# Late-search counts and the attention's squares: from VectorE to ScalarE

## The chip, the cores and the metric

The kernel runs as one program on one core of one Trainium2 chip. The metric is the device time of one execution in microseconds (us). Before the change it is 2590.02 us, the median of three runs (2584.93 to 2590.75). A core has five engines that run side by side, each with its own instructions in a fixed order: TensorE (PE, with its weight loads listed as PEld), VectorE (DVE), ScalarE (ACT), GpSimd (POOL), and SyncE (SP), which issues the DMAs.

## The reference, cut to what matters

A decoder layer over 2048 tokens of width 1024. One input projection feeds two groups of heads: sparse attention (8 heads of 64, one shared key and value head) and a short gated convolution. Both are normalised head by head, projected out and merged into the residual; a SwiGLU FFN follows. The change touches two places of the attention. A small indexer scores every earlier key, and each query keeps the 256 keys of highest score:

```python
score = jnp.where(causal[None], score, NEG_INF)
_, sel = lax.top_k(score, k_sel)          # k_sel = 256
...
xf = xf * lax.rsqrt(jnp.mean(jnp.square(xf), axis=-1, keepdims=True) + EPS)   # attention's output, per head
```

## The kernel before

The 2048 queries are 16 blocks of 128, one query to a partition. Block b has (b+1) x 128 causal keys. Blocks 0 and 1 need no selection. For the others `topk` finds, for each query, the threshold of the 256th largest score, by a search: eight rounds (`NITER`) count how many scores are at or above a trial value and move one end of an interval to it, and a last part takes the exact value out of the few that remain (L550 to L567, on VectorE, with one copy on ScalarE and a DMA of the mask `u` to DRAM).

Blocks are searched in groups: `GROUPS` = (2 to 5), (6 to 8), (9, 10) while the projections run, and `LATE` = (11, 12, 13), (14, 15) later, beside the attention. In a round, each block's columns are cut in two. ScalarE takes the last `n2` columns (L512: Sign of the trial value minus the score, with an accumulated sum per partition, `ca2`), VectorE the first `n1 = n - n2` (L514: is_ge, with an accumulated count, `cd`). `n2` is one number for a group: 58% of the group's mean width, rounded down to 64. For the late groups it is 960 and 1088, so that VectorE has 576, 704, 832 and 832, 960 columns. L517 on VectorE adds both engines' counts, and some ten small operations on 128x3 or 128x2 values give the next trial value `tc` (L518 to L546), for which both engines' next counts wait.

The attention walks over the blocks in the order `ORDER` (2, 4, 7, 0, 10, 1, 9, 3, 8, 5, 6, 11, 13, 12, 15, 14) and within a block over its key tiles. A step of `weigh` makes, for two groups of four heads, three matmuls (L888 to L890) into a PSUM tile `l` (two buffers), an exponential (L894, ScalarE), its half-precision copy `ph` (L895, ScalarE) and the rest `pr` (L896, GpSimd); `values` then makes 24 small matmuls (L906 to L908). Ahead of a block, `maxima` multiplies queries and keys (L863) into PSUM tiles `m` (four buffers) and VectorE reduces them with the mask (L865). After a block, `finish` copies the output to SBUF (L912, ScalarE), squares it (L915, VectorE), sums the squares per head (L917) and scales; `mix` transposes it, multiplies by the output weights (L946), and normalises, with the transposes of the normalised rows `z` at L964.

The late search is the attention's background job: one step of its generator is emitted at each attention step, and a block of `LATE` must be settled before its maxima are emitted. When it is done, the same generator goes on with the first FFN weights (`after_late`, which calls `prep_w`: loads `wg` and `wu`, combinations of them on GpSimd from L1092 on), into space that the search's pools give back. The order in which each engine gets its instructions is made by a planner that simulates a timeline when the kernel is built (`schedule_with_timeline_sim=True`); emission order and `tc.high_priority` set priorities in it. So an edit of durations can move other instructions.

Of the kernel before, what the change touches and what calls it, by code (L numbers as in the profile page):

```python
# [13 lines left out]
BF16 = mybir.dt.bfloat16  # L14
I32 = mybir.dt.int32
AF = mybir.ActivationFunctionType
ALU = mybir.AluOpType
# [4 lines left out]
P = 128  # L22
# [35 lines left out]
DVE_SHARE = 0.42  # L58
GROUPS = [(2, 3, 4, 5), (6, 7, 8), (9, 10)]
LATE = [(11, 12, 13), (14, 15)]  # L60
# [82 lines left out]
def body(ctx: ExitStack, tc: tile.TileContext, A, out, force=False):  # L143
# [314 lines left out]
    def topk(blocks, scs):  # L458
        nb = len(blocks)
        b0 = blocks[0]  # L460

        def sm(name, k=1):
            return tk.tile([P, k, nb], F32, tag=f"{name}", name=f"{name}{b0}", bufs=2)

        def cst(c):
            return ct[:, c + b0:c + b0 + nb]

        st6 = tk.tile([P, nb, 6], F32, tag="st6", name=f"st6_{b0}")
        mv = tk.tile([P, nb, 2], F32, tag="mv", name=f"mv_{b0}")
        for i in range(nb):  # L470
            m = 2 * TOPK if blocks[i] >= 4 else TOPK
            head = tk.tile([P, 2 * TOPK], F32, tag="sp", name="head")[:, 0:m]
            S_.activation(head, scs[i][:, 0:m], AF.Copy, scale=1.0 / SS2)
            V.bn_stats(st6[:, i], head)
            V.bn_aggr(mv[:, i], st6[:, i])
            yield
        mu, sd = sm("mu")[:, 0], sm("sd")[:, 0]
        rsqrt(V, tk, sd, mv[:, :, 1], 1e-30)
        V.scalar_tensor_tensor(sd, sd, SS2, mv[:, :, 1], op0=ALU.mult, op1=ALU.mult)
        V.tensor_scalar(mu, mv[:, :, 0], SS2, None, op0=ALU.mult)  # L480
        tcur = sm("tc", 2)

        ends = tk.tile([P, 2, 2, nb], F32, tag="ends", name=f"ends{b0}", bufs=2)
        lo, hi = ends[:, 0], ends[:, 1]
        a, f = sm("a")[:, 0], sm("f")[:, 0]
        which, upper = sm("which", 2), sm("upper", 2)
        cd, ca2 = sm("cd")[:, 0], sm("ca2")[:, 0]
        t = tcur[:, 0]
        cnt = tcur[:, 1]
        V.tensor_tensor(a, sd, cst(C_Z), op=ALU.mult)  # L490
        V.tensor_tensor(t, a, mu, op=ALU.add)
        V.scalar_tensor_tensor(lo[:, 0], sd, -6.0, mu, op0=ALU.mult, op1=ALU.add)
        V.scalar_tensor_tensor(hi[:, 0], sd, 8.0, mu, op0=ALU.mult, op1=ALU.add)
        zero, below = sm("zero")[:, 0], sm("below")[:, 0]

        n2 = int(sum(b + 1 for b in blocks) / nb * P * (1 - DVE_SHARE)) // 64 * 64
        big_at, tgt = TOPK - n2 / 2.0, TGT - n2 / 2.0
        V.tensor_scalar(lo[:, 1], cst(C_N), -n2 / 2.0, None, op0=ALU.add)
        V.memset(hi[:, 1], -n2 / 2.0)
        G.memset(zero, 0.0)  # L500
        G.memset(below, -2100.0)
        G.memset(upper[:, 0], 0.0)
        G.memset(upper[:, 1], 1.0)
        dd = sm("dd", 2)
        yield
        for it in range(NITER):
            for i, b in enumerate(blocks):
                n = (b + 1) * P
                n1 = n - n2
                j1 = tk.tile([P, 1024], BF16, tag="j1", name="j1", bufs=1)  # L510
                j2 = tk.tile([P, 1216], BF16, tag="j2", name="j2", bufs=1)
                S_.activation(j2[:, 0:n2], scs[i][:, n1:n], AF.Sign, bias=t[:, i:i + 1],  # L512
                              scale=-1.0, accum_out=ca2[:, i:i + 1])
                V.tensor_scalar(j1[:, 0:n1], scs[i][:, 0:n1], t[:, i:i + 1], None,  # L514
                                op0=ALU.is_ge, op1=ALU.add, accum_out=cd[:, i:i + 1])
                yield
            V.scalar_tensor_tensor(cnt, ca2, -0.5, cd, op0=ALU.mult, op1=ALU.add)  # L517
            V.scalar_tensor_tensor(which, tcur[:, 1:2].broadcast_to([P, 2, nb]), big_at, upper,  # L518
                                   op0=ALU.is_ge, op1=ALU.not_equal)
            V.copy_predicated(ends, which.bitcast(I32).unsqueeze(2).broadcast_to([P, 2, 2, nb]),  # L520
                              tcur.unsqueeze(1).broadcast_to([P, 2, 2, nb]))
            if it == NITER - 1:
                break
            V.tensor_tensor(dd, hi, lo, op=ALU.subtract)
            d = dd[:, 0]
            if it == 0:
                V.scalar_tensor_tensor(a, cnt, -tgt, sd, op0=ALU.add, op1=ALU.mult)
                V.tensor_tensor(a, a, cst(C_SL), op=ALU.mult)
                V.tensor_tensor(a, a, t, op=ALU.add)
                V.scalar_tensor_tensor(f, d, 0.02, lo[:, 0], op0=ALU.mult, op1=ALU.add)  # L530
                V.tensor_tensor(a, a, f, op=ALU.max)
                V.scalar_tensor_tensor(f, d, -0.02, hi[:, 0], op0=ALU.mult, op1=ALU.add)
                V.tensor_tensor(t, a, f, op=ALU.min)
            else:
                V.reciprocal(a, dd[:, 1])
                V.scalar_tensor_tensor(f, lo[:, 1], -tgt, a, op0=ALU.add, op1=ALU.mult)
                V.tensor_scalar(f, f, CLIP - 1.0, -CLIP, op0=ALU.max, op1=ALU.min)
                V.tensor_tensor(f, f, d, op=ALU.mult)
                V.tensor_tensor(t, lo[:, 0], f, op=ALU.subtract)
            if it == PROBE:  # L540
                V.tensor_scalar(a, lo[:, 0], 0.0, None, op0=ALU.is_lt)
                V.scalar_tensor_tensor(f, hi[:, 0], 0.0, a, op0=ALU.is_gt, op1=ALU.mult)
                V.copy_predicated(t, f.bitcast(I32), zero)
            if it == PROBE + 1:
                V.tensor_scalar(f, hi[:, 0], 0.0, None, op0=ALU.is_equal)
                V.copy_predicated(t, f.bitcast(I32), below)  # L546
            yield
        r, thr, m8 = sm("rk")[:, 0], sm("thr")[:, 0], tk.tile([P, nb, 8], F32, tag="m8", name=f"m8{b0}")
        ri = tk.tile([P, nb], I32, tag="ri_", name=f"ri{b0}")
        V.tensor_scalar(ri, hi[:, 1], n2 / 2.0 + 0.25, None, op0=ALU.add)  # L550
        V.tensor_scalar(r, ri, -1.0, float(TOPK), op0=ALU.mult, op1=ALU.add)
        for i, b in enumerate(blocks):
            n = (b + 1) * P
            sp = tk.tile([P, S], F32, tag="sp", name="sp", bufs=1)
            V.tensor_scalar(sp[:, 0:n], scs[i], hi[:, 0, i:i + 1], 2.0 * NEG, op0=ALU.is_ge, op1=ALU.mult)
            V.tensor_tensor(sp[:, 0:n], sp[:, 0:n], scs[i], op=ALU.add)
            yield
            V.max(m8[:, i], sp[:, 0:n])
            pick = tk.tile([P, 8], F32, tag="pick", name="pick")
            V.scalar_tensor_tensor(pick, ct[:, C_IOTA:C_IOTA + 8], r[:, i:i + 1], m8[:, i], op0=ALU.is_equal,  # L560
                                   op1=ALU.mult, accum_out=thr[:, i:i + 1])
            yield
            u = tk.tile([P, S], BF16, tag="u", name="u", bufs=1)
            V.tensor_scalar(u[:, 0:n], scs[i], thr[:, i:i + 1], None, op0=ALU.is_lt, op1=ALU.add,
                            accum_out=flag[:, b:b + 1])
            S_.activation(u[:, 0:n], u[:, 0:n], AF.Copy, scale=NEG)
            dma(u_d[b - 2], u[:, 0:n])  # L567
            yield
# [252 lines left out]
    def attention(pool=None, background=None, at_block=None, at_end=None):  # L821
# [88 lines left out]
        def finish(b, po):  # L910
            ov = aq[0].tile([P, 2, 4, 65], F32, tag="ov", name=f"ov{b}", bufs=two)
            S_.activation(ov, po[:, :, 0:260].rearrange("p g (h d) -> p g h d", d=65), AF.Copy)  # L912
            o3 = ov.rearrange("p g h d -> p (g h) d")
            sq = aq[0].tile([P, H, DH], F32, tag="asq", name=f"asq{b}", bufs=1)
            V.tensor_tensor(sq, o3[:, :, 0:64], o3[:, :, 0:64], op=ALU.mult)  # L915
            ms = ap.tile([P, 2, H], F32, tag="ms", name=f"ms{b}", bufs=2)
            V.tensor_reduce(ms[:, 0], sq, axis=AX.X, op=ALU.add)  # L917
            V.tensor_tensor(ms[:, 1], o3[:, :, 64], o3[:, :, 64], op=ALU.mult)
            V.scalar_tensor_tensor(ms[:, 0], ms[:, 1], EPS * DH, ms[:, 0], op0=ALU.mult, op1=ALU.add)
            root(ap, ms[:, 0], ms[:, 0], 1.0 / DH, None)  # L920
            on = ap.tile([P, H, DH], F32, tag="on", name=f"on{b}", bufs=three)
            V.tensor_tensor(on, o3[:, :, 0:64], ms[:, 0].unsqueeze(2).broadcast_to([P, H, DH]), op=ALU.mult)
            return on
# [710 lines left out]
```

## Time and profile before

| | us |
|---|---|
| median of three runs | 2590.02 |
| the profiled execution | 2585.36 |
| its span, first to last instruction | 2583.5 |
| PE busy | 2335.9 (90%) |
| DVE busy | 1835.4 (71%) |
| ACT busy | 1185.9 (46%) |
| POOL busy | 1184.6 (46%) |

Busy times are over the whole span; the stages differ much. The mean granted clock of TensorE is 0.956 of full speed. In a row, the letters before an operation name the engine; `out<-in` are the program's tile names; "x" is a number of instructions. A wait is written as who waited, an arrow, and what it waited for.

### The profile page before, as it was taken

How to read it: one execution, taken by the hardware profiler on the slowest of the kernel's cores; microseconds unless marked ns; L12 is line 12 of the kernel's file. 1: busy time of each engine (PE TensorE's matmuls, PEld its weight loads, DVE VectorE, ACT ScalarE, POOL GpSimd, SP SyncE). 2: the span in 40 equal slices, each digit the busy share in tenths (PEclk: the TensorE clock that was granted, in tenths of full speed). 3: DMA queues.
4: the chain of work that ended last, by engine and by line, in shares of the span. 5: the costliest groups of instructions: out<-in, count | busy, mean ns of one | idle time of the engine just before them, and what ended most of it. 6: DMA issues, size and time to landing. Idle time of an engine off the chain costs nothing. (4 is left out here: it accounts for less than half of the span.)

```text
span 2583.5 us, 38131 instructions
## 1 busy us (share of the span) xinstructions
PE 2335.9 (90%) x13538; PEld 1126.0 (44%) x13538; DVE 1835.4 (71%) x3649; ACT 1185.9 (46%) x2263; POOL 1184.6 (46%) x960
## 2 busy tenths in 40 slices
PE   6799999996878799889969999999999996999998
PEld 3444444443444355445524444444444442444443
DVE  8998999989999877774377676666666687422223
ACT  3687776546766556667643333233323343110000
POOL 3000000004444655786555665565555664855445
PEclk8899999997988899999989999999999997999999
DMA  7321442433131422331233222222223236444443
GB/s 267 130 101 68 144 136 89 161 132 111 59 108 49 145 80 71 106 115 45 84 116 102 90 86 74 76 72 78 86 75 88 87 106 200 149 138 149 131 134 123
DMA packets 213913, 281.69 MB, mean 109 GB/s; under 512 B 15824, under 2 KB 128848, under 8 KB 212944
## 3 DMA queue, kind: packets, MB, share of 16 engines
q1 hardware_dynamic: 213712, 279.17, 33.9%
q8 instruction: 107, 1.75, 0.3%
q14 instruction: 94, 0.77, 0.1%
HBM read 183.20 MB, written 95.91 MB: 108 GB/s over the span
## 5 line engine op out<-in xcount | busy, mean ns | idle before, releaser
L1206 PE MATMUL f<-h,wwg 128*128 128x512 f16 x1800 | 418.8, 383 | 26.5 <-ACT h L1169 19.9
L896 POOL TENSOR_TENSOR pr<-p,ph 128x512 f16<-128x512 f32 x272 | 330.8, 1233 | 218.1 <-ACT ph L895 160.4
L1206 PE MATMUL f<-h,wwu 128*128 128x512 f16 x1800 | 413.5, 379 | 0.0
L1502 PEld LDWEIGHTS <-gi 128*128 128x128 f16 x1848 | 181.5, 99 | 276.1 <-DMA gi<-gg_d 44.8
L1240 POOL TENSOR_TENSOR go<-g,go 128x512 f16<-128x512 f32 x126 | 169.6, 1356 | 275.2 <-ACT go L1239 235.1
L1206 PEld LDWEIGHTS <-wwu 128*128 128x128 f16 x1848 | 180.8, 98 | 234.4 <-issue 17.3
L1206 PEld LDWEIGHTS <-wwg 128*128 128x128 f16 x1848 | 181.8, 99 | 232.0 <-issue 14.1
L1502 PE MATMUL f<-wdo,gi 128*128 128x512 f16 x1032 | 241.9, 387 | 14.9 <-DMA gi<-gg_d 6.9
L865 DVE CUSTOM_DVE_ANT_0 jk<-m,ua 128x512 bf16<-128x512 f32 (+3 forms) x320 | 193.7, 605 | 71.9 <-PE m L863 56.1
L894 ACT ACTIVATE p<-l 128x512 f32<-128x512 f32 x272 | 157.3, 596 | 91.1 <-PE l L890 82.6
L1239 ACT ACTIVATE go<-g 128x512 f16<-128x512 f32 x132 | 82.4, 627 | 230.7 <-issue 82.8
L447 ACT ACTIVATE r<-xs 128x512 f32<-128x512 f32 (+3 forms) x304 | 153.5, 547 | 59.2 <-PE xs L446 15.4
L895 ACT ACTIVATE ph<-p 128x512 f16<-128x512 f32 x272 | 166.1, 632 | 3.9 <-PE o L908 0.8
L1502 PE MATMUL f<-wdr,gi 128*128 128x512 f16 x576 | 136.8, 386 | 16.7 <-DVE g L1213 8.8
L737 PE MATMUL b<-hi,wch 128*128 128x512 f16 x384 | 146.8, 382 | 0.0
L737 PE MATMUL b<-lo,wch 128*128 128x512 f16 x384 | 146.6, 382 | 0.0
L737 PE MATMUL b<-hi,wcl 128*128 128x512 f16 x384 | 146.3, 381 | 0.0
L908 PE MATMUL o<-vst,pr 128*128 128x65 f16 x1088 | 136.1, 197 | 9.3 <-POOL pr L896 9.1
L906 PE MATMUL o<-vst,ph 128*128 128x65 f16 x1088 | 138.7, 195 | 3.1 <-ACT ph L895 2.0
L863 PE MATMUL m<-k1T,qst 128*128 128x512 f16 (+3 forms) x320 | 109.2, 372 | 35.6 <-DVE mp L865 31.5
L907 PE MATMUL o<-vst,ph 128*128 128x64 f16 x1088 | 138.5, 195 | 0.0
L1469 ACT ACTIVATE frs<-fmv,epsw 128x1 f32<-128x1 f32 x16 | 4.7, 295 | 281.7 <-DVE fmv L1466 281.7
(384 smaller groups left out, 5247.2 us busy)
## 6 DMA issues: line engine op xcount, KB each, us to landing
gg_d<-go SPq DMA_DIRECT2D x154, 256.0 KB, 2.6
gi<-gg_d SPq DMA_DIRECT2D x112, 256.0 KB, 3.0
wa<-in_w_ada SPq DMA_DIRECT2D x64, 256.0 KB, 2.9
wg<-in_wg SPq DMA_DIRECT2D x49, 256.0 KB, 2.9
wu<-in_wu SPq DMA_DIRECT2D x49, 256.0 KB, 3.0
wd<-in_wd SPq DMA_DIRECT2D x44, 256.0 KB, 3.0
gi<-gg_d SPq DMA_DIRECT2D x56, 192.0 KB, 2.8
wa<-in_w_ada SPq DMA_DIRECT2D x16, 512.0 KB, 8.6
```

The source lines that it names most:

```text
L447: S_.activation(r[:, i:i + e], ps[:, 0:e], AF.Relu)
L737: T.matmul(ps, w[:, k, j * P:(j + 1) * P], x[:, k], start=n == 0, stop=n == 3 * KT - 1)
L865: V.tensor_tensor_reduce(jk[:, 0:w], ps[:, 0:w], u[:, j * 512:j * 512 + w], scale=1.0, scalar=-3e38, op0=ALU.add, op1=ALU.max, accum_out=m ...
L894: S_.activation(p32, pl_, AF.Exp, scale=DH ** -0.5)
L895: S_.activation(ph, p32, AF.Copy)
L896: G.tensor_tensor(pr, p32, ph, op=ALU.subtract)
L906: T.matmul(o, lhs, vst[:, kt, 64:129], start=kt == 0 and hh == 0, stop=False)
L907: T.matmul(o[:, 0:64], lhs, vst[:, kt, 0:64], start=False, stop=False)
L908: T.matmul(o, pr[:, hh * P:(hh + 1) * P], vst[:, kt, 64:129], start=False, stop=kt == b and hh == 3)
L1206: T.matmul(ps, w[:, x, k * P:(k + 1) * P], h[:, y, :, k], start=n == 0, stop=n == 11)
L1240: (V if (p, grp) in LASTG else G).tensor_tensor(o[:, :, 1], x4, o[:, :, 0], op=ALU.subtract)
L1502: T.matmul(ps, g[:, p - p0, x], wd_tiles[m, p][:, y], start=p == 0 and n == 0, stop=p == NP - 1 and n == 2)
```

## The change

In `topk`, for the groups of `LATE` alone, `n2` becomes the first block's number times 128: 1408 for (11, 12, 13) and 1792 for (14, 15). ScalarE so counts the last 1408 or 1792 columns of each block, and VectorE the first 128, 256, 384 (blocks 11, 12, 13) and 128, 256 (blocks 14, 15). The widths of the two scratch outputs `j1` and `j2` follow; the earlier groups keep their cuts. In `finish`, the square of the attention's output is made by ScalarE with the function Square, where VectorE multiplied the tile by itself.

```diff
-        n2 = int(sum(b + 1 for b in blocks) / nb * P * (1 - DVE_SHARE)) // 64 * 64
+        if blocks in LATE:
+            n2 = b0 * P
+        else:
+            n2 = int(sum(b + 1 for b in blocks) / nb * P * (1 - DVE_SHARE)) // 64 * 64
...
-                j1 = tk.tile([P, 1024], BF16, tag="j1", name="j1", bufs=1)
-                j2 = tk.tile([P, 1216], BF16, tag="j2", name="j2", bufs=1)
+                j1 = tk.tile([P, 640], BF16, tag="j1", name="j1", bufs=1)
+                j2 = tk.tile([P, 1792], BF16, tag="j2", name="j2", bufs=1)
...
-            V.tensor_tensor(sq, o3[:, :, 0:64], o3[:, :, 0:64], op=ALU.mult)
+            S_.activation(sq, o3[:, :, 0:64], AF.Square)
```

## Rows read from the trace of the kernel before

**Rows 1.** One line's instructions: count, duration ns min/median/max, first and last start us.
```profile
L512 ACT ACTIVATE j<-scb,tc x40: 1082/1100/1277, 611.3 to 827.2; 128x960 bf16<-128x960 f32 x24, 128x1088 bf16<-128x1088 f32 x16
...
L566 ACT ACTIVATE u<-u x14: 522/1213/1910, 240.0 to 857.4; 128x384 bf16<-128x384 bf16 x1, 128x512 bf16<-128x512 bf16 x1, 128x640 bf16<-128x640 bf16 x1, 128x768 bf16<-128x768 bf16 x1
```

**Rows 2.** Stretches: us; busy us (x instructions) of PE, PEld, DVE, ACT, POOL; clock; DMA.
```profile
605.00:857.00 252.00, 198.48 (x1718) 107.78 (x1716) 238.58 (x632) 170.82 (x337) 125.37 (x103) 0.89 0.24 80
857.00:890.00 33.00, 22.39 (x82) 10.14 (x83) 26.83 (x69) 14.52 (x29) 15.84 (x12) 0.73 0.47 152
890.00:1290.00 400.00, 360.76 (x3569) 206.79 (x3568) 252.46 (x578) 264.44 (x537) 259.24 (x215) 0.98 0.26 88
```

**Rows 3.** Chain that ended last, first piece from 560 us on: start us, us.
```profile
1321.74 1.57 DVE g L1215
```

**Rows 4.** Waits of PE, 605 to 857 us: us in total, times, longest.
```profile
PE m L863 <- DVE mp L865: 14.7, 20, 1.8
PE l L888 <- ACT p L894: 9.4, 14, 1.5
PE m L964 <- DVE z L956: 8.2, 2, 4.7
PE o L908 <- POOL pr L896: 6.5, 10, 2.1
PE m L875 <- DVE mx L871: 6.5, 3, 3.2
PE m L875 <- DVE mx L873: 2.6, 2, 1.6
```

**Rows 5.** Groups of DVE, by shape, 180 to 870 us: busy, mean ns, idle before.
```profile
L514 DVE TENSOR_SCALAR_CACHE_REDUCE j<-scb,tc 128x832 bf16<-128x832 f32 x16 | 17.2, 1073 | 0.2
...
L514 DVE TENSOR_SCALAR_CACHE_REDUCE j<-scb,tc 128x960 bf16<-128x960 f32 x8 | 9.7, 1209 | 0.1
...
L514 DVE TENSOR_SCALAR_CACHE_REDUCE j<-sc,tc 128x320 bf16<-128x320 f32 x16 | 8.6, 540 | 0.2
...
L514 DVE TENSOR_SCALAR_CACHE_REDUCE j<-scb,tc 128x704 bf16<-128x704 f32 x8 | 7.5, 938 | 0.0
...
L514 DVE TENSOR_SCALAR_CACHE_REDUCE j<-scb,tc 128x576 bf16<-128x576 f32 x8 | 6.5, 808 | 0.1
...
L514 DVE TENSOR_SCALAR_CACHE_REDUCE j<-sc,tc 128x192 bf16<-128x192 f32 x8 | 3.3, 409 | 0.2
...
L514 DVE TENSOR_SCALAR_CACHE_REDUCE j<-sc,tc 128x64 bf16<-128x64 f32 x8 | 2.2, 274 | 0.1
```

**Rows 6.** Groups of ACT, by shape, 180 to 870 us.
```profile
L512 ACT ACTIVATE j<-scb,tc 128x960 bf16<-128x960 f32 x24 | 26.3, 1097 | 11.3 <-DVE tc L539 5.7 <-DVE tc L546 4.5 <-DVE tc L491 0.8
L512 ACT ACTIVATE j<-scb,tc 128x1088 bf16<-128x1088 f32 x16 | 19.4, 1210 | 16.5 <-DVE tc L539 5.8 <-DVE tc L491 4.3 <-DVE tc L546 3.5
...
L754 ACT ACTIVATE g<-y 128x512 f32<-128x512 f32 x16 | 10.0, 628 | 14.2 <-DVE y L753 14.2
...
L512 ACT ACTIVATION_READ_ACCUMULATOR j<-scb,tc 128x1 f32 x40 | 7.8, 196 | 0.0
...
L566 ACT ACTIVATE u<-u 128x1792 bf16<-128x1792 bf16 x1 | 1.7, 1697 | 0.0
...
L566 ACT ACTIVATE u<-u 128x1408 bf16<-128x1408 bf16 x1 | 1.4, 1377 | 1.4 <-DVE u L564 1.4
```

**Rows 7.** The square: line L915 in the whole span, then its group in 605 to 857 us.
```profile
L915 DVE TENSOR_TENSOR asq<-ov x16: 675/687/1635, 622.0 to 1279.4; 128x512 f32<-128x512 f32 x16
...
L915 DVE TENSOR_TENSOR asq<-ov 128x512 f32<-128x512 f32 x7 | 7.3, 1040 | 0.0
```

**Rows 8.** The sum of a round's counts, groups of DVE by shape, 605 to 857 us.
```profile
L517 DVE SCALAR_TENSOR_TENSOR tc<-ca,cd 128x3 f32<-128x3 f32 x8 | 3.5, 437 | 0.0
...
L517 DVE SCALAR_TENSOR_TENSOR tc<-ca,cd 128x2 f32<-128x2 f32 x8 | 1.2, 154 | 0.3 <-ACT j L512 0.3
```

**Rows 9.** Waits of POOL, 605 to 890 us.
```profile
POOL wg L1092 <- DMA wg<-in_wg: 15.5, 1, 15.5
```

## The prediction

> **What bounds the kernel now.** I read the table of stretches first, because the two edited statements live in one stretch: the counts of blocks 11 to 15 run from 611.3 to 827.2 us and the copy of their last selection starts at 857.4 us [rows 1]. The reader is to see in [rows 2] that from 605 to 857 us VectorE is busy 238.6 of 252 us (0.947) while TensorE has 198.5, ScalarE 170.8 and GpSimd 125.4: VectorE is the full engine here and nowhere later. From 890 to 1290 us TensorE has 360.8 of 400 and VectorE 252.5, so there TensorE is the bound. The chain of waits from the end is no help for this stretch: its first piece shown begins at 1321.74 us [rows 3], and everything before it is order on the engines. So I take TensorE's own idle time instead. In the stretch it is 252 - 198.5 = 53.5 us, and the waits [rows 4] name most of it: for VectorE 14.7 + 8.2 + 6.5 + 2.6 = 32.0 us (score maxima whose PSUM bank is not free yet, and normalised rows and maxima that are late for their transposes), for ScalarE and GpSimd 9.4 + 6.5 = 15.9 us (the exponentials and their rests). What the stage gains or loses is read from these two sums. Later stages are carried by TensorE's work, which the change leaves alone, so an end of the stage that is earlier by some us should reach the end of the kernel as such.
>
> **What the change removes from VectorE.** The counts of the late search are 8 rounds of 5 blocks. Now their 40 instructions take 17.2 + 9.7 + 7.5 + 6.5 = 40.9 us [rows 5]. A column costs (1209 - 808)/(960 - 576) = 1.04 ns. After, the widths are 128, 256, 384 for the first group and 128, 256 for the second. Between the rows for 64, 192 and 320 columns, and 64 columns beyond the last, that is 342, 475 and 607 ns, so 8 x (0.342 + 0.475 + 0.607) + 8 x (0.342 + 0.475) = 11.4 + 6.5 = 17.9 us. Removed: 23.0 us. The squares are 16, of which 7 fall into the stretch and cost 7.3 us there [rows 7]. Removed in the stretch: 30.3 us of 238.6, 12.7%.
>
> The square alone takes 687 ns (the median), in the stretch it averages 1040 ns and reaches 1635 [rows 7]; so 7 x 0.35 = 2.5 us of the 7.3 is not work. The same is to be seen at the first operation behind a round's counts: 437 ns for three columns while GpSimd is busy, 154 ns for two columns [rows 8]. The Trainium skill, SBUF — State Buffer, section "SBUF: two separate sides", explains it: a VectorE instruction with two SBUF inputs and a GpSimd instruction take one shared port in turn, each for its whole length. By bare durations the sum would lose 4.8 us of squares, by that rule the full 7.3, which is what the rows show. The rule also speaks against the change: a count has one SBUF input, so moving counts away frees no port, and the small two-input steps of the search stay as long as they are.
>
> **What it adds to ScalarE.** Now 26.3 + 19.4 = 45.7 us of counting [rows 6]. A count of 1408 or 1792 columns is not in the trace. Below, the copies of the same widths, 1377 and 1697 ns; above, the step from 960 to 1088 columns (113 ns for 128, 0.88 ns a column) carried on, 1492 and 1832 ns. At 960 the count stands about 90 ns over where the copies would be, so I take 1475 and 1800 ns: 24 x 1.475 + 16 x 1.800 = 64.2 us, added 18.5 us (14.5 to 19.4). The accumulator read of 196 ns stays, 40 times. A square of this very shape stands in the convolution, 628 ns [rows 6]: 7 x 0.63 = 4.4 us in the stretch, 5.6 after it. ScalarE goes from 170.8 to 193.7 us, VectorE from 238.6 to 208.3. Neither is then full in 252 us; TensorE's 198.5 lies between them.
>
> **What that is worth to TensorE.** Bounds: if VectorE alone paced the stretch, the whole 30.3 us goes, and with a granted clock of 0.98 as later in place of 0.89 [rows 2] a little more, some -32; if waits shrink only as the load does, 12.7% of 32.0, -4.1. I take half of 32.0, -16.0, for this reason: what a maximum or a small step stands behind on VectorE is most often a count, today 0.81 to 1.21 us long, afterwards 0.34 to 0.61, half. On ScalarE an exponential stands behind a count of 1.10 to 1.21 us plus 0.20, later 1.475 to 1.80 plus 0.20, 1.3 to 1.45 times as long; 15.9 us times 0.38 is +6.0 (between 0 and the added 22.9). Sum for the stretch: -10.0 us.
>
> The square's move adds no hop: ScalarE writes the copy of the output and now squares it right behind; VectorE's reduction waits for ScalarE where the multiply waited before. Between a square's length less and as much more each time, taken at 0 because the multiply is hidden by TensorE from 890 us on (8 x 0.687 = 5.5 us [rows 7] off an engine with 147 us idle, 5.0 us onto ScalarE with 136 us idle [rows 2]). If that cover were gone the later half would move by -5.5 to +5.
>
> Behind the search the planner puts the first FFN weights. GpSimd stands 15.5 us for the first of them [rows 9], with the attention's rests queued behind it, and TensorE has 22.4 of 33 us at a granted clock of 0.73 from 857 to 890 us [rows 2]. The load waits for space that the search gives back, so an earlier or later end of the search moves it along with the stage. I count 0, with -10 (TensorE's idle 10.6 gone) and +10 (as much again) as bounds. The two scratch tiles go from 4480 to 4864 bytes a partition; each is written by one engine alone, so they add no wait: 0.
>
> **How this stands to the time.** The profiled execution took 2585.4 us, 4.6 below the median of 2590.0 of the runs. 2585.4 - 10.0 = 2575.4 in its own terms (its span of 2583.5 us and the 1.9 us around it that the change does not touch); set against the median, 2590.0 - 10.0 = 2580.0, which I predict.
>
> **Rivals.**
> *VectorE paces everything:* the stage shrinks with its load, -18 to -32, so 2558 to 2572. For it: 0.947 busy. Against: ScalarE would then have 193.7 of some 221 us, in one queue with counts of 2 us, and the 15.9 us of TensorE's waits on that side would not stay.
>
> *Slower: VectorE stands for ScalarE's counts.* The place is the first operation behind a round's counts, which needs both engines' sums. Today a round is 3 x (1.097 + 0.196) = 3.9 us on ScalarE against 3.1 on VectorE (three counts and their reads), in the second group 2.8 against 2.4: at most 16 x 0.6, about 10 us exposed, and 0.3 us of it shows [rows 8]. After, it is 5.0 against 1.7, and 4.0 against 1.0: 8 x 3.3 + 8 x 3.0 = 50 us, 40 more. Queued behind that operation are the maxima, on which TensorE waits. If all 40 were exposed: -30.3 + 40 + 6.0 = +16, 2606; it decides from about 30 us exposed, three quarters. For it: ScalarE takes the counts in its own order, with exponentials between, and lags. Against: only 3% of today's exposure shows, because maxima stand between count and sum, and ScalarE has 11.3 + 16.5 = 27.8 us in which it waits for the next threshold [rows 6], which comes sooner from a lighter VectorE.
>
> *No change:* half of that exposure (20 us) and ScalarE's +6.0 eat the 30.3; between -7 and +7, 2583 to 2597. For it: the search remains a chain of eight rounds whose longer leg is now ScalarE's, 1.1 us longer in each of 16 rounds (17.6 us), and the port waits stay. That the edit does not do what it says I give nothing: widths and engine are fixed by it.
>
> **Chances.** The forecast (-5 to -17, so 2573 to 2585) 0.42, VectorE pacing everything 0.15, no change 0.25, slower 0.18. A measurement of this kernel tells 0.3% from no change, 7.8 us: faster is then below 2582.2, slower above 2597.8. Of the forecast's 0.42 some 0.35 lies below 2582.2; with 0.15 that is 0.50 faster, 0.32 the same, 0.18 slower. The range for 8 in 10 goes from 2560 (into the first rival, which also covers half of the -10 at the weights) to 2600 (the start of the slower one). For the likeliest case alone it is 2570 to 2589.
>
> **What would show it.** In the profile after: the 40 late counts on VectorE near 18 us and on ScalarE near 64; 16 squares of 0.63 us on ScalarE; VectorE near 208 us and ScalarE near 194 in the stretch from the start of the late search to its last result, and that stretch some 242 us long; TensorE's waits for VectorE there near 16 us, those for ScalarE and GpSimd near 22. The slower rival would show as VectorE idle for ScalarE at the sum of the counts, of 10 us or more. The forecast is wrong if the stretch keeps its 252 us although VectorE lost 30 us, if GpSimd's wait for the first weights grows, or if the later stretch, which I left alone, changes by more than 5 us.

## The result: 33 us faster, and where they were

The median went from 2590.4 to 2557.2 us (four runs each, 2584.9 to 2592.7 and 2554.6 to 2560.0); the ratio is 0.9875, with a 95% interval of 0.9856 to 0.9894. The forecast was 2580 with a range from 2560: right in direction, too small by a factor of three, and the time lies below the range. The profiled execution has a span of 2554.8 us, 28.7 less than before.

First the tables of stretches of the changed kernel, with the columns of [rows 2].

```profile
605.00:857.00 252.00, 208.66 (x1847) 114.27 (x1847) 218.40 (x669) 199.28 (x368) 124.23 (x107) 0.94 0.25 84
857.00:890.00 33.00, 26.99 (x225) 14.98 (x224) 29.34 (x54) 22.73 (x43) 20.11 (x17) 0.90 0.43 144
890.00:1290.00 400.00, 357.64 (x3396) 200.81 (x3394) 249.08 (x559) 259.19 (x524) 252.46 (x207) 0.97 0.27 92
605.00:900.00 295.00, 242.64 (x2149) 133.17 (x2148) 255.91 (x740) 228.41 (x424) 154.26 (x131) 0.94 0.28 95
...
605.00:1335.20 730.20, 617.12 (x5559) 339.96 (x5558) 541.98 (x1320) 502.30 (x970) 434.61 (x353) 0.94 0.27 93
```

In the first row TensorE has done 1847 matmuls in the same 252 us, 129 more than in [rows 2], at a granted clock of 0.94 in place of 0.89. VectorE has fallen from 238.6 to 218.4 us, ScalarE has risen from 170.8 to 199.3. The last row ends where the FFN's unbroken run of matmuls begins. That point is the first number of these pieces of the chain of waits (start, length), before and after:

```profile
1362.12 706.85 PE f L1206 x3263
```

```profile
1335.20 705.74 PE f L1209 x3263
```

It comes 26.9 us earlier; what follows keeps its length to 2 us. From 605 us to that point the kernel before has, in the same columns:

```profile
605.00:900.00 295.00, 228.80 (x1863) 122.02 (x1862) 274.65 (x714) 193.68 (x384) 150.54 (x121) 0.87 0.28 92
...
605.00:1362.12 757.12, 627.23 (x5563) 344.72 (x5562) 573.09 (x1335) 478.97 (x954) 439.30 (x355) 0.93 0.27 90
```

TensorE's work is the same (5563 and 5559 matmuls in the records). Its idle time went from 757.1 - 627.2 = 129.9 to 730.2 - 617.1 = 113.1 us, 16.8 less, and its busy time from 627.2 to 617.1, 10.1 less. The second goes with the clock at which the same matmuls ran: from 605 to 900 us the granted clock is 0.87 before and 0.94 after. With two levels, full and half, 0.87 is about 77 us at the lower one and 0.94 about 35 us. From 900 us to the FFN, before and after, a part of this is given back, at 0.96 and 0.94:

```profile
900.00:1362.12 462.12, 398.43 (x3701) 222.70 (x3700) 298.44 (x622) 285.29 (x571) 288.76 (x235) 0.96 0.26 88
```

```profile
900.00:1335.20 435.20, 374.48 (x3410) 206.79 (x3410) 286.07 (x581) 273.89 (x547) 280.35 (x223) 0.94 0.27 91
```

So 17 us are stalls that went, and 10 us are matmuls that ran faster on balance. That the second follows from the first is not shown: two kernels below lose stalls and gain no clock up to the FFN.

The two edits themselves came out as worked out. Groups by shape, 605 to 900 us: the counts on VectorE, the sum of a round's counts, then the counts and the squares on ScalarE.

```profile
L517 DVE TENSOR_SCALAR_CACHE_REDUCE j<-scb,tc 128x256 bf16<-128x256 f32 x16 | 7.6, 474 | 0.2
L517 DVE TENSOR_SCALAR_CACHE_REDUCE j<-scb,tc 128x128 bf16<-128x128 f32 x16 | 5.5, 342 | 0.3
...
L517 DVE TENSOR_SCALAR_CACHE_REDUCE j<-scb,tc 128x384 bf16<-128x384 f32 x8 | 4.8, 606 | 0.0
...
L517 DVE DVE_READ_ACCUMULATOR j<-scb,tc 128x1 f32 x40 | 3.2, 81 | 0.0
...
L520 DVE SCALAR_TENSOR_TENSOR tc<-ca,cd 128x3 f32<-128x3 f32 x8 | 2.9, 365 | 2.4 <-ACT j L515 2.4
L520 DVE SCALAR_TENSOR_TENSOR tc<-ca,cd 128x2 f32<-128x2 f32 x8 | 2.2, 270 | 4.5 <-ACT j L515 4.5
```

```profile
L515 ACT ACTIVATE j<-scb,tc 128x1408 bf16<-128x1408 f32 x24 | 35.3, 1470 | 5.0 <-DVE tc L542 2.4 <-DVE tc L546 0.9 <-DVE tc L549 0.9
L515 ACT ACTIVATE j<-scb,tc 128x1792 bf16<-128x1792 f32 x16 | 28.6, 1788 | 13.9 <-DVE tc L491 4.9 <-DVE tc L549 3.7 <-DVE tc L542 3.6
...
L918 ACT ACTIVATE asq<-ov 128x512 f32<-128x512 f32 x8 | 5.1, 635 | 0.1
```

VectorE's counts are 17.9 us, as forecast, ScalarE's 63.9 (64.2 forecast), and a square is 0.635 us. VectorE now does stand for ScalarE's counts, as the slower rival had it, but for 2.4 + 4.5 = 6.9 us, not for 30.

The search itself did not become shorter. ScalarE's counts and its copies of the selections, in the changed kernel:

```profile
L515 ACT ACTIVATE j<-scb,tc x40: 1452/1474/1803, 610.0 to 843.8; 128x1408 bf16<-128x1408 f32 x24, 128x1792 bf16<-128x1792 f32 x16
...
L569 ACT ACTIVATE u<-u x14: 523/1212/1910, 238.5 to 873.5; 128x384 bf16<-128x384 bf16 x1, 128x512 bf16<-128x512 bf16 x1, 128x640 bf16<-128x640 bf16 x1, 128x768 bf16<-128x768 bf16 x1
```

In [rows 1] the last of these start at 827.2 and 857.4 us. The last selection comes 16 us later than before, and the kernel is faster all the same: by 900 us TensorE has done 2149 matmuls since 605 us where it had done 1863. What got ahead is the attention, not the search beside it.

TensorE's waits in 605 to 857 us (in total, times, longest), against [rows 4], and GpSimd's wait for the first FFN weights in 605 to 890 us, against [rows 9]:

```profile
PE m L866 <- DVE mp L868: 13.9, 21, 2.3
PE l L891 <- ACT p L897: 7.9, 11, 2.9
PE m L878 <- DVE mx L874: 5.5, 3, 4.5
PE o L911 <- POOL pr L899: 5.0, 7, 1.5
PE m L967 <- DVE z L959: 3.2, 3, 2.3
PE m L878 <- DVE mx L876: 2.8, 1, 2.8
```

```profile
POOL wg L1095 <- DVE wwg L216: 1.0, 1, 1.0
```

The waits for ScalarE and GpSimd did not grow, they fell from 15.9 to 12.9 us, although ScalarE has 28 us more to do in the stretch. GpSimd's wait of 15.5 us is gone. It looks like the reason: in the planned order 104 of GpSimd's rests `pr` now stand ahead of the first weights where 88 stood, and the copy of block 8's output (L912, now L915) comes 35 us earlier:

```profile
934.51 0.60 ACT L912 ACTIVATE ov<-o 128x520 f32<-128x520 f32 x1
```

```profile
899.56 0.60 ACT L915 ACTIVATE ov<-o 128x520 f32<-128x520 f32 x1
```

The experiments had to tell this place in the order from VectorE's load.

### The profile page after: what moved, and what is told of

Same layout as the page of the kernel before. It is cut to its first block, busy times and chain, and to the rows that moved or that the text cites. A ratio compares the mean times of both kernels' runs of the same rounds, so it can differ in the third digit from the quotient of the medians.

```text
span 2554.8 us, 38117 instructions
## 1 busy us (share of the span) xinstructions
PE 2323.3 (91%) x13538; PEld 1120.6 (44%) x13538; DVE 1802.5 (71%) x3633; ACT 1209.3 (47%) x2279; POOL 1180.9 (46%) x960
## 4 chain that ended last, share of the span: by engine, by line
PE 32%; POOL 7%; DMA 5%; DVE 4%; issue 2%; ACT 0%; SPq 0%; DVEq 0%; POOLq 0%; ACTq 0%
PE f L1209 28%; PE f L1505 4%; DMA x<-xn_d 2%; POOL z L1482 1%; POOL x L1492 1%; POOL x L1493 1%; DMA gi<-gg_d 1%; POOL z L1549 1%; POOL z L1550 1%; DMA wd<-in_wd 1%; DVE wdr L216 1%; DVE wdo L216 1%; DVE h L1173 0%; DVE z L1538 0%; POOL wd L1114 0%
## 5 line engine op out<-in xcount | busy, mean ns | idle before, releaser
L1209 PEld LDWEIGHTS <-wwg 128*128 128x128 f16 x1848 | 182.0, 99 | 231.8 <-issue 13.9
```

Of the source, the lines that this page charges most:

```text
L1209: T.matmul(ps, w[:, x, k * P:(k + 1) * P], h[:, y, :, k], start=n == 0, stop=n == 11)
```

## The experiments

All ratios are to the kernel before, run beside it on the same chip; the brackets are 95% intervals.

**Each edit alone.** `count_only` is the changed kernel with the multiplication back on VectorE, `square_only` the kernel before with

```diff
-            V.tensor_tensor(sq, o3[:, :, 0:64], o3[:, :, 0:64], op=ALU.mult)
+            S_.activation(sq, o3[:, :, 0:64], AF.Square)
```

> The new cut of the late counts alone; the square stays on VectorE. Theory A (VectorE's load: the stage shrinks by what VectorE is spared): 23 of the 30 us go, so about 25 of the 33 us gained, near 2565 us. Theory B (the planned order: by the end of the search more attention steps stand ahead of GpSimd's first instruction on the FFN weights, 103 of its rests in place of 88, so that it no longer waits for the DMA): nearly the whole gain, 2555 to 2562 us, and GpSimd's wait of 15.5 us for the first weights is gone.

> The square on ScalarE alone; the cut of the counts stays. The order puts 88 of GpSimd's rests ahead of the first FFN weights, as before the change. Theory A: VectorE is spared 7 us in the stage, near 2583 us. Theory B: 2587 to 2593 us, and GpSimd's wait of about 15 us stays.

Measured: counts alone 0.9957 [0.9940, 0.9975], 2575.2 us; squares alone 0.9931 [0.9909, 0.9953], 2569.6 us. Both theories missed. The counts, with the order that B wanted, gave less than half of what A or B expected; the squares, with the old order, gave 17 us where 7 were expected at most. Together they are near the whole (11 + 17 of 33). From 605 us to the FFN's unbroken run of matmuls, first `count_only`, then `square_only`:

```profile
605.00:1355.96 750.96, 632.14 (x5558) 348.71 (x5558) 546.54 (x1336) 495.68 (x954) 436.24 (x353) 0.91 0.27 90
605.00:1350.34 745.34, 629.97 (x5559) 345.11 (x5558) 557.70 (x1317) 486.76 (x969) 434.73 (x354) 0.92 0.27 91
```

TensorE's idle time falls from 129.9 to 118.8 and 115.4 us, most of what the whole change takes away, but its busy time rises from 627.2 to 632.1 and 630.0, with the granted clock at 0.91 and 0.92 against 0.93. Fewer stalls did not bring a higher clock here. The last selection's copy starts at 879.0 us in `count_only` and at 851.5 in `square_only`: it is the counts that lengthen the search.

**VectorE keeps the counts; the weights wait by themselves.** `both_high` adds to `count_only`, behind VectorE's count:

```diff
+                if blocks in LATE:
+                    n3 = {11: 448, 14: 704}[b0]
+                    V.tensor_scalar(j1[:, 0:n3], scs[i][:, n1:n1 + n3], t[:, i:i + 1], None,
+                                    op0=ALU.is_ge, op1=ALU.add, accum_out=cd3[:, i:i + 1])
```

`gate8` leaves the kernel before as it is, and holds the first six weight loads back until block 8 is done (`gate8` is a column that VectorE writes from block 8's output):

```diff
+            S_.activation(t[:, 0:1], gate8, AF.Copy)      # ahead of the first six loads into their tiles t
```

> The new cut alone, and VectorE besides counts the columns that went to ScalarE once more into a scratch tile whose sum nobody reads: VectorE keeps the work of before (about 41 us and 40 instructions more), ScalarE has the new work. The planned order comes out as in the new cut alone (103 rests ahead of the first weights). Theory A: nothing is gained, 2587 to 2600 us. Theory B: most of the gain stays, 2557 to 2570 us.

> The kernel before, but the first six loads of FFN weights wait (by one small ScalarE copy each into their tiles) until block 8 of the attention is done; 115 of GpSimd's rests stand ahead of the first instruction on these weights, and the order up to the end of the search is that of before. Theory A (VectorE's load): the wait of 15.5 us was only the place where VectorE's lateness showed, 2585 to 2592 us. Theory B (the order behind the search): the wait goes and 10 to 25 us with it, 2565 to 2580 us.

Measured: `both_high` 0.9979 [0.9968, 0.9991], 2581.5 us; `gate8` 0.9999 [0.9986, 1.0012], 2587.8 us. `both_high` lies between the two theories; `gate8` is as A had it, and with it theory B falls. In `gate8` GpSimd's longest-wait rows in 605 to 890 us hold no wait for the weights any more:

```profile
POOL pr L896 <- ACT ph L895: 99.1, 27, 12.9
POOL mx L869 <- PE m L875: 36.8, 6, 17.2
POOL pr L896 <- issue: 5.0, 1, 5.0
```

and the time is what it was: the 15.5 us were the place at which lateness showed, not its cause. `both_high` has the same 103 rests ahead as `count_only` and ScalarE's whole new work, and half of that kernel's gain. Its rows: the repeated counts on VectorE and the stretch of 605 to 900 us, then that from 605 us to the FFN.

```profile
L522 DVE TENSOR_SCALAR_CACHE_REDUCE j<-scb,tc 128x448 bf16<-128x448 f32 x24 | 16.2, 675 | 0.2
L522 DVE TENSOR_SCALAR_CACHE_REDUCE j<-scb,tc 128x704 bf16<-128x704 f32 x16 | 15.0, 940 | 0.2
```

```profile
605.00:900.00 295.00, 235.56 (x2038) 130.01 (x2038) 279.93 (x800) 219.09 (x399) 141.07 (x119) 0.90 0.25 84
...
605.00:1357.19 752.19, 625.63 (x5558) 345.73 (x5558) 579.42 (x1416) 495.24 (x954) 436.75 (x353) 0.92 0.27 90
```

VectorE is back at 279.9 of 295 us (31.2 us of repeated counts, more than the 23 that had been moved), and TensorE's idle time is back at 126.6 us, from 118.8 in `count_only`. The half of the gain that stayed lies within what plans scatter by (below). ScalarE at 219.1 costs nothing that can be seen.

**The squares.** `square_dup` squares on ScalarE and lets VectorE multiply the same tile into `on`, which is overwritten later; the other two give ScalarE the squares of the first or of the last eight blocks of the order alone.

```diff
+            S_.activation(sq, o3[:, :, 0:64], AF.Square)
+            V.tensor_tensor(on, o3[:, :, 0:64], o3[:, :, 0:64], op=ALU.mult)   # square_dup
...
+            if ORDER.index(b) < 8 and pool is not None:                        # sq_first8; >= 8: sq_last8
```

> ScalarE squares as in the run of the square alone (2569.6 us, 17 us gained), and VectorE multiplies the same tile besides, into a tile that is overwritten later: VectorE keeps its 16 operations. The order ahead of the first FFN weights is the same (88 rests). Theory A (VectorE's load): the gain is lost, 2584 to 2592 us. Theory B (what moves in the planned order, or the shorter way from copy to square on one engine): the gain stays, 2567 to 2575 us.

> The square on ScalarE for the first 8 blocks of the attention's order alone (the ones beside the late search), counts as before. Theory A1 (VectorE is the full engine beside the search, and only there): most of the 17 us of the square, 2570 to 2576 us. Theory A2 (TensorE also waits for VectorE's chains later): a third or less, 2580 to 2585 us.

> The square on ScalarE for the last 8 blocks alone, after the search. Theory A1: nothing, 2585 to 2590 us. Theory A2: 8 us or more of the 17, 2572 to 2580 us.

Measured: `square_dup` 0.9993 [0.9980, 1.0006]; `sq_first8` 0.9940 [0.9924, 0.9957]; `sq_last8` 0.9953 [0.9937, 0.9969]. With VectorE's operations kept the gain is nil: it lies in what VectorE's multiplications cost, not in ScalarE's shorter way from copy to square. Whether that is VectorE's own time or also what the multiplications and GpSimd's instructions cost each other, the run does not separate, for both came back. The repeated ones cost nearly what the old ones did in 605 to 857 us (7.3 us, [rows 7]), and TensorE's idle time from 605 us to the FFN is 129.1 us again:

```profile
L917 DVE TENSOR_TENSOR on<-ov 128x512 f32<-128x512 f32 x7 | 6.5, 932 | 0.0
...
605.00:1363.63 758.63, 629.52 (x5558) 346.14 (x5557) 576.31 (x1332) 486.47 (x969) 437.72 (x353) 0.92 0.26 89
```

A1's number for the later eight, nothing, is missed: they gained nearly as much as the first eight. But the two parts add up to 1.07% where the whole is 0.69%, and a kernel below (`minus64`) gains as much with more work on VectorE, so the price of the later eight is not shown. TensorE does wait there for the end of VectorE's chains. The row of L964 in the kernel before, and of the same line in `sq_last8`, both 900 to 1290 us:

```profile
L964 PE MATMUL m<-ct,z 128*128 128x128 f32 x72 | 12.6, 298 | 15.8 <-DVE z L956 15.8
```

```profile
L967 PE MATMUL m<-ct,z 128*128 128x128 f32 x80 | 13.6, 292 | 11.5 <-DVE z L959 11.5
```

**Both old works put back; half the step; a step further; a cut disturbed.** `after_counts_dup` and `after_dup` are the changed kernel with the additions of `both_high`, and of both. The others:

```diff
+            n2 = {11: 1184, 14: 1440}[b0]          # after_half, in place of b0 * P
...
+            S_.activation(z, z, AF.Identity, scale=rs, bias=nm)   # after_half_z: nm = -mean * rs, made by VectorE
...
+        n2 -= 64 * (blocks in LATE)                # minus64, in the kernel before
```

> The changed kernel with half of the step in the cut: ScalarE counts 1184 and 1440 columns in place of 1408 and 1792; the squares on ScalarE. If the gain goes with the columns that VectorE is spared, it lies half way between the square alone (2570) and the changed kernel (2557), near 2563 us. If it hangs on where the FFN weights stand in the order (101 rests ahead of them here, 104 in the changed kernel, 88 before), it is 2555 to 2560 us, and it could be better than the changed kernel, since ScalarE is less loaded.

> The changed kernel, and VectorE besides counts the columns that went to ScalarE once more into a scratch tile whose sum nobody reads; the squares are on ScalarE. 106 of GpSimd's rests stand ahead of the first FFN weights (104 in the changed kernel). Theory A (what VectorE is spared): only the squares' gain stays, and what the same kernel kept without the squares (5 us), 2564 to 2572 us. Theory B (the planned order and the denser TensorE): 2555 to 2561 us.

> The changed kernel with both of VectorE's old works besides: the counts of the old widths into scratch, and the multiplication of the attention's output into a tile that is overwritten later. ScalarE has all the new work too. Theory A: 2580 to 2588 us, little of the 32 us is left. Theory B: 2555 to 2568 us.

> The kernel before with the late cut moved by 64 columns towards VectorE (896 and 1024 for ScalarE): VectorE gets 2.7 us more, ScalarE 2.1 us less. It asks how far the time moves when the planner is merely disturbed. If by load alone: 2587 to 2590 us. If each new plan throws the time by several us: outside 2582 to 2592.

> A further step the same way: half of the cut's step (2555.7 us), the squares on ScalarE, and the normalisation of the rows z (16 VectorE operations of 0.8 to 1.6 us, for which TensorE's transposes wait longest in the later half) on ScalarE as scale and bias, with one small VectorE operation more each. If VectorE's load still sets the pace after the change: 2543 to 2551 us. If ScalarE or the longer way (a hop more between the engines) now counts: 2555 to 2565 us.

Measured: `after_half` 0.9876 [0.9860, 0.9893], 2555.7 us: the second half of the step adds nothing. It falls on the number that the theory of the order gave, but `gate8` speaks against that theory. Whether VectorE's load stops paying before the full step, or the plan hides the 6 us that load alone gave the second half, this run does not say. `after_counts_dup` 0.9970 [0.9956, 0.9984], 2579.4 us: more is lost than the counts' part, 8 us are left where A's 2564 to 2572 us left 13 to 21; `after_dup` 0.9978 [0.9966, 0.9990], 2579.1 us, so that with VectorE's old work back 6 of 33 us remain, 1 us more than A's range allows. Its TensorE idles 125.7 us between 605 us and the FFN, against 113.1 in the changed kernel:

```profile
605.00:1355.67 750.67, 624.98 (x5558) 343.94 (x5557) 571.73 (x1411) 502.23 (x969) 434.66 (x353) 0.93 0.26 90
```

`after_half_z` 0.9897 [0.9880, 0.9914], 2558.2 us: 16 operations of 0.8 to 1.6 us less on VectorE (and a small one more each) bring nothing on top. `minus64` 0.9952 [0.9936, 0.9968], 2575.2 us: with *more* work on VectorE it is 10 us faster than the kernel before. Load alone cannot do that; what else the edit can change is the plan. So single differences of up to 10 us in this study can be the plan.

**How far plans scatter.** Six neighbours: the cut at +64 (`plus64`, `sq_plus64`), -64 and -128 (`sq_minus64`, `minus128`) from the old place, half the step without the squares (`half_only`), and 64 columns short of the new place (`after_m64`). The edits are those above with another number.

> The kernel before with the late cut moved by 64 columns towards ScalarE (1024 and 1152), squares on VectorE. By load: -1 to -2 us, 2584 to 2588. If a new plan throws the time by some 5 to 10 us whichever way the load goes (as in the run with 64 columns the other way, 10 us faster with more VectorE work): anywhere in 2574 to 2592.

> Half of the cut's step (1184 and 1440 columns for ScalarE), squares on VectorE. By load, half of the whole step's 11 us: near 2581 us. If the counts' part is within the scatter of plans: anywhere in 2570 to 2590.

> Squares on ScalarE, and the cut 64 columns towards VectorE (896 and 1024). If the squares on ScalarE are worth 17 us by what they spare: near 2571 us. If 10 us of that was a lucky plan: 2575 to 2582 us.

> The changed kernel with the cut 64 columns back (1344 and 1728 columns for ScalarE). If the changed kernel's 32 us are its load: 2556 to 2560 us. If a lucky plan is in it: 2562 us or more.

> Squares on ScalarE, and the cut 64 columns towards ScalarE (1024 and 1152). By load: 2567 to 2570 us. With a scatter of plans of some 5 us: 2562 to 2578.

> The kernel before with the cut 128 columns towards VectorE (832 and 960 for ScalarE), squares on VectorE: VectorE gets 5.3 us more. By load: 2589 to 2595 us. By scatter of plans alone: 2574 to 2592.

| ratio to before | cut near the old place | cut near the new place |
|---|---|---|
| squares on VectorE | -128: 1.0024 [1.0014, 1.0035]; -64: 0.9952; 0: 1; +64: 0.9990 [0.9979, 1.0000] | half: 0.9905 [0.9889, 0.9922]; full: 0.9957 |
| mean | 0.9992 | 0.9931 |
| squares on ScalarE | -64: 0.9948 [0.9932, 0.9965]; 0: 0.9931; +64: 0.9943 [0.9926, 0.9960] | half: 0.9876; full - 64: 0.9920 [0.9898, 0.9941]; full: 0.9875 |
| mean | 0.9941 | 0.9890 |

The half steps lie between the two places and are counted to the new one. Within a corner plans differ by up to 0.7%, 19 us from end to end. Between corners the squares are worth 0.9992 - 0.9941 = 0.51%, 13 us, the counts 0.61%, 16 us (with the squares on ScalarE 0.51% as well, 13 us), both 1.02%, 26 us. The spread inside the corners (a standard deviation of 0.26%, from these twelve kernels) leaves each price uncertain by 5 to 6 us: the whole is well clear of that, the two parts less so, and neither is known to be the larger. TensorE's idle time between 605 us and the FFN's unbroken run, taken in each trace as above, agrees: it is 120.2 to 133.6 us in the four kernels with the squares on VectorE and the cut near its old place, 110.2 to 121.9 in the eight of the other corners, and 125.1 to 129.1 in the five controls named next. From the first corner's mean to the last one's it falls by 14.5 us (128.0 to 113.5); the rest of the 26 is mostly shorter busy time.

The four kernels with the load of VectorE at or near its old size and another plan (`both_high`, `square_dup`, `after_dup`, `gate8`) lie at 0.9978 to 0.9999, `after_counts_dup`, with the squares alone spared, at 0.9970, above its corner. The kernel measured as the change lies 0.15% below the mean of its corner, and the kernel before 0.08% above that of its own, 6 us together.

## Why the prediction was too small

Three steps failed: the price put on ScalarE's side, the path by which a shorter stretch was to reach the end, and the granted clock that the sum left out. One more, the waits for VectorE, was mis-sized.

- *What bounds the stretch*: right in part. VectorE's work is part of what TensorE lacks; `both_high`, `square_dup` and `after_dup` show it by putting that work back (idle time to the FFN 118.8 to 126.6, 115.4 to 129.1 and 113.1 to 125.7 us). But that a shorter stretch would hand its earlier end on to the kernel failed: I expected some 242 us from the search's start to its last result, and the last selection came 16 us later. The search lengthened by about what the rival "no change" gave ScalarE's longer leg (17.6 us), yet the kernel got faster.
- *What is removed and added*: right to a few tenths of a us, counts and squares, on both engines. (One square is left out of the sum: with seven in the stretch nine lie behind it, not eight.) VectorE has 218.4 us in the stretch and not 208.3, ScalarE 199.3 and not 193.7; TensorE did 129 matmuls more there.
- *Half of TensorE's 32.0 us of waits for VectorE go, -16.0*: this term was mis-sized. The named waits for VectorE in the stretch went from 32.0 to 13.9 + 5.5 + 3.2 + 2.8 = 25.4 us, -6.6, though TensorE did more work in that time. All idle time of the stretch fell from 53.5 to 43.3 us; that these -10.2 us are the forecast's sum of -10.0 is luck, with -6.6 for -16.0 and -3.0 for +6.0. Another 6.6 us went behind 857 us, where I had put nothing. My reason, that maxima stand behind counts, is not borne out: their waits are 14.7 and 13.9 us.
- *+6.0 us on ScalarE's side*: this failed. I scaled waits with the length of the count that stands in front. They fell by 3.0, and kernels with ScalarE's added work and VectorE's old one lose nothing against the kernel before. ScalarE had 81 us to spare in the stretch.
- *The eight later squares at nothing, hidden by TensorE's 360.8 of 400 us*: open. `sq_last8` gained 0.47%, but `minus64` gained 0.48% with nothing taken from VectorE, so neither zero nor 12 us is shown. The reason was too weak in any case: a mean share of 0.9 is no proof of cover when the engine's remaining idle time holds waits for just that chain (15.8 us at L964).
- *The shared port*: the squares came out at 13 us for 15 us spared, the counts at 16 for 23. The small steps of the search stayed as they were: a median of 156 ns before and 164 after, and a few long ones, up to 1437 and 1240 ns; the 437 ns of [rows 8] is a mean that two long ones of eight make. By the Trainium skill, SBUF — State Buffer, section "SBUF: two separate sides", the squares, with two inputs, could hold a port that GpSimd needs; an operation with one input does so only in a two-port mode. The long steps, and the old squares of up to 1635 ns [rows 7], agree with it; the difference of the two prices is within the scatter, so no run here shows it.
- *The granted clock*: left out of the sum and named only as "a little more" in a rival. It goes with 10.1 us of the 26.9, the largest term left out. The mean over the whole span is 0.961 to 0.963 in the changed kernel's four runs and 0.958 to 0.964 in `after_half`'s, against 0.956 in the profile before; in `count_only` and `square_only` it is 0.955 to 0.958 and 0.954 to 0.960, and their gains are the smaller ones, though they had lost 11.1 and 14.5 us of idle time where the changed kernel lost 16.8. Why the one plan earns it and the other not is open.
- *The first FFN weights at 0*: right as a price (`gate8`), though the wait did vanish.
- *The rivals*: "VectorE paces everything", 2558 to 2572 us at a chance of 0.15, came nearest in number; the stage that it had shrink did not end earlier. The slower one's mechanism is there with 6.9 us of 50. A rival was missing: that a new plan moves the time by itself, by up to 10 us either way, load or no load. It should have widened the range at the lower end too.

## What to carry to other kernels

Here one engine was near full in a stretch and the one that took over its work stood at two thirds. The time that it was spared, there and later, was worth about 0.7 of itself (26 us for some 38, give or take 5), and the engine that took the work over cost nothing that can be seen up to 0.79 of the stretch (199 of 252 us); do not charge its longer instructions to the path without a row that shows that path late. A background job may end later while the work it stands beside gets ahead: read the gain from that work. Count TensorE's busy time beside its idle time: at equal work the first moved too, by -10 us in the changed kernel and +5 in `count_only`. Where a planner lays out the whole program, measure neighbours of a change before a single part of it is credited with less than a per cent.

## What the runs showed of the hardware

ScalarE's count with an accumulated sum costs (1788 - 1470)/384 = 0.83 ns a column, VectorE's (606 - 342)/256 = 1.03 ns, plus a read of the sum of 0.196 and 0.081 us. At 960 columns both take 1.29 us with their reads ([rows 5], [rows 6]); on longer rows ScalarE is the faster counter of the two. I had not expected the granted clock to go with more than a third of the gain. In the changed kernel the granted clock of 605 to 900 us rose from 0.87 to 0.94 while TensorE's idle time there fell by 14 us (66.2 to 52.4); in `count_only` it fell by 13 us (to 53.0) and the clock rose to 0.90 alone.
